# TensorE's instructions of five attention heads in a written order, with float32 values, an undivided attention map and transposed spreads

## The chip, the cores and the metric

One core of a Trainium2 chip runs the whole program as one launch. The metric is device time in microseconds (us), lower is better. Engines are named as the profile names them: PE is TensorE's matmul, PEld its weight load, DVE is VectorE, ACT is ScalarE, POOL is GpSimd, SPq is the queue of SyncE from which nearly all transfers are issued.

## The reference, cut to what matters

Two layers work on 512 tokens of width 1024. Layer 0 mixes with differential attention and a Fourier transform, layer 1 with a short convolution; after each comes a mixture of 16 experts that take 64 tokens each. What the change touches is the attention of layer 0 (6 heads, each with two maps of 64 channels, 768 keys of which 256 are context) and the vectors that modulate each layer (ada, 6 of 1024 per layer):

```python
s = jnp.einsum('bqhmd,bkhmd->bhmqk', q, k)
p = jax.nn.softmax(s, axis=-1)
a = p[:, :, 0] - lam * p[:, :, 1]
att = jnp.einsum('bhqk,bkhe->bqhe', a, v)
...
att = rmsnorm(att, subln) * (1.0 - lam_init)
o = jnp.concatenate([att, fourier_mix(f)], axis=-1)
return o @ w_out
...
sh_m, sc_m, g_m, sh_f, sc_f, g_f = split(silu(c) @ w_ada + b_ada)
```

## The kernel before, in words

The program runs in stages: the input and the first modulation (to about 94 us), heads 0 to 4 (about 94 to 344 us), head 5 with the output projection (to about 410 us), the choice of tokens for the experts (to about 449 us), experts of layer 0 (to 905 us), convolution and its choice of tokens (to 1145 us), experts of layer 1 (to 1608 us).

Matmuls of precision are written in two ways. A float32 matmul is one call of `mm` (L68) and stands in the trace as two PE instructions. `mm3` (L257) is three fp32r matmuls, each one instruction, on operands that `split` (L247 to L255) has cut into a high part (a cast on ACT, L250) and a low part (a difference on DVE, L251). A PE transpose is one instruction.

The head loop (`attention`, from L622) goes over `h` in 0 to 5 and over `i` in 0 to 3, the blocks of 128 queries; while head h is attended, head H = h+1 is projected. One round of `i` holds:
- `maxexp` (L461): for each of the two maps a DVE maximum over 768 keys (L466) and an ACT exponential (L467), which also gives the sums `su`.
- `proj(H, tt)`, two calls in each of the rounds 0 to 2: 24 fp32r matmuls of 384 columns (256 for the two context tiles), then `proj_fin` (L399): a square on ACT (L404), the split of v (L250, L251), the rotation on DVE (L409, L413, L424), the sum (L420), the root on POOL (L87, L88) and the product on POOL (L426).
- `scores(h, i+1)` (L450): 12 fp32r matmuls on half the rows of the array.
- `normalise` (L471): `lam / su1` on DVE, the second map scaled on ACT (L475), the first scaled and the second subtracted on DVE (L476).
- `proj_tr(H, i-1)` (L437): 4 transposes (2 for the context pair) of projected q and k, then splits.
- `att_tr` (L481): 6 transposes of the map, then `split` into `ah` and `al`.
- after odd rounds `values` (L494): 18 fp32r matmuls of 256 columns; in the next round `subnorm` (L506) sums the squares with matmuls against ones and takes the root on POOL, and `subscale` (L515) spreads the result over the partitions by a float32 matmul of a broadcast column with the identity.
- after round 3 the weights of head H+1 are loaded and split (`wsplit_head`); after heads 0 and 1 also `fourier` (L555): 8 float32 matmuls of 256 columns, a copy on ACT, 2 float32 matmuls of 512 columns.
- one step of `ada_steps` (L185): parts of a modulation vector (a load, ACT L170, DVE L174, POOL L176) and, after four parts, `ada_sum` (L178): 8 float32 matmuls of one column against ones.

No order is written: Tile's scheduler puts every engine's instructions in one fixed order at build time, by priority (the order of the program, shifted for ada parts by AP) and its own estimate of times. On the chip each engine works that order down, so an instruction that waits holds all behind it on its engine. Two banks of PSUM serve the tag `pj` (projections), two the tag `tr` (transposes, values, sums), four the scores. The tiles of a head's q, k and v come from the pool `qkv` with four slots, two for each head; head H takes the two that head h-1 had. The experts' weights are loaded from SPq into slots of several pools in a written cycle (`CYC`), among them the slots that attention gives back.

`gate_row` (L214) spreads a gate vector over the partitions with 8 float32 matmuls; it is called for both output projections and both choices of tokens.

Of the kernel before, what the change touches and what calls it, by code (L numbers as in the profile page):

```python
# [24 lines left out]
S = 512  # L25
# [17 lines left out]
def body(ctx: ExitStack, tc: tile.TileContext, t, out):  # L43
# [22 lines left out]

    def mm(o, l, r, start, stop):
        return T.matmul(o, l, r, start=start, stop=stop, skip_group_check=True)  # L68
# [47 lines left out]
    lam = cst.tile([128, 1], F32, name="lam")  # L116
# [14 lines left out]
    def small_params(raw, raw2):  # L131
# [13 lines left out]
        V.scalar_tensor_tensor(lam, le[:, 0:1], LAM0, le[:, 1:2], op0=ALU.add, op1=ALU.subtract)  # L145
# [32 lines left out]
    def ada_sum(l, w, acc):  # L178

        b = bank("tr", None)  # L180
        for k in range(KD):
            mm(b[:, k:k + 1], acc[:, k * 128:k * 128 + 128], one1, True, True)
        V.tensor_tensor(adaT[l, 0][:, w, :], b[:, :KD], biasT[:, l, w, :], op=ALU.add)

    def ada_steps(params, steps, new):  # L185

# [3 lines left out]
        for step in range(steps):  # L190
            while n < len(todo) and n * steps < (step + 1) * len(todo):
                l, w, j = todo[n]
                n += 1
                if j == 0:
                    if acc is not None:
                        ada_sum(*todo[n - 2][:2], acc)
                    acc = new()
# [4 lines left out]
        ada_sum(*todo[-1][:2], acc)  # L202
# [11 lines left out]
    def gate_row(l, which, pool_, after=None):  # L214

        dst = pool_.tile([128, D], F32, name=f"gate{l}{which}")
        for q in range(2):
            b = bank("tr", None)
            for k in range(4):
                m = mm(b[:, k * 128:k * 128 + 128],  # L220
                       adaT[l, 0][:, 2 + 3 * which, 4 * q + k:4 * q + k + 1].to_broadcast([128, 128]), ident,
                       True, True)
# [41 lines left out]
    def attention():  # L264
# [40 lines left out]
        sing = tabs.tile([128, NT, 2, 2, 64], F32, name="sing")  # L305
        gk1 = tabs.tile([128, 64], F32, name="gk1")
        gx_ = tabs.tile([128, 2, 64], F32, name="gx")

        def table_loads(st):
            gb = st.tile([128, 2, 64], F32, name="gb")  # L310
            SP.dma_start(out=cosg[:, :, 1, :], in_=t["cos"].rearrange("(a p) d -> p a d", p=128))
            SP.dma_start(out=sing[:, :, 1, 1, :], in_=t["sin"].rearrange("(a p) d -> p a d", p=128))
# [6 lines left out]
        def tables(gb):  # L319
            V.tensor_copy(gk1, gb[:, 1, :])  # L320
            V.tensor_scalar(gb[:, 0, :], gb[:, 0, :], 0.125, None, op0=ALU.mult)
            for b in range(4):
                V.tensor_copy(gx_[:, :, 16 * b:16 * b + 16], gb[:, :, 16 * (b ^ 1):16 * (b ^ 1) + 16])
            for j in range(2):
# [3 lines left out]
                for m in range(2):  # L328
                    V.tensor_tensor(sing[:, :, j, m, :], sing[:, :, 1, 1, :],
                                    gx_[:, j, None, :].to_broadcast([128, NT, 64]), op=ALU.mult)  # L330
# [56 lines left out]
        def new_head(h):  # L387
            a, b = [qkv.tile([128, 2048], F32R, tag="w", name=n) for n in ("qk", "qv")]
# [92 lines left out]
        def att_tr(h, i, p):  # L481
            if i % 2 == 0:
                AT[0] = [ap_.tile([128, 6, 256], F32R, tag=f"a{x}", name=f"a{x}") for x in "hl"]
# [869 lines left out]
```

## Time and profile before

| | |
|---|---|
| runs of the kernel before | 1604.41, 1606.08, 1611.53 us; median 1606.08 us |
| profiled execution | 1609.78 us; its span from first to last instruction 1608.0 us |
| busy share of the span | PE 94%, PEld 56%, DVE 42%, ACT 24%, POOL 14% |
| mean granted clock of TensorE | 0.979 |
| read from HBM | 491.41 MB |

The span is what the trace shows; the time of the execution has 1.8 us more around it. A busy PE is not a PE at its peak, since ends of matmuls are modelled and overlap; the distance from one start to the next tells what an instruction costs in a stream. The granted clock is 1.00 at 2.4 GHz and 0.50 at 1.2 GHz.

### The profile page before, as it was taken

The numbers are of one execution on the slowest core, as the hardware profiler recorded it, in microseconds if no ns is written. First come the engines' busy times: TensorE is split into PE (matmuls) and PEld (weight loads), VectorE is DVE, ScalarE is ACT, GpSimd is POOL, SyncE is SP. The second block draws the span as 40 slices with busy tenths as digits, with TensorE's granted clock in tenths as the row PEclk, the third lists the DMA queues.
The fourth block names the chain that finished last, engine by engine and source line by source line (L and its number), as shares of the span: only waits on it lengthen the run. The fifth ranks groups of instructions, "written<-read, shape, count | busy, mean of one in ns | idle before, by whom it ended". The sixth has DMA issues, their size and how long they took to land. (4 is left out here: it accounts for less than half of the span.)

```text
span 1608.0 us, 19864 instructions
## 1 busy us (share of the span) xinstructions
PE 1517.4 (94%) x7936; PEld 898.3 (56%) x7936; DVE 677.1 (42%) x1336; ACT 388.0 (24%) x753; POOL 225.3 (14%) x234
## 2 busy tenths in 40 slices
PE   4989999888999999999999899999899999999997
PEld 2978888777544444444443487887444444444443
DVE  3868788897612122112212567463312221221222
ACT  4535565553111001000100444232110010010000
POOL 0334355553000000000000024311000000000000
PEclk9889999999999999999999999999999999999999
DMA  9533444462799999999999766437999999999997
GB/s 346 168 103 106 156 136 155 158 236 104 302 364 360 410 409 409 409 409 409 409 409 404 265 209 209 157 131 271 348 399 399 409 409 409 410 408 409 409 409 278
DMA packets 162778, 494.79 MB, mean 308 GB/s; under 512 B 11750, under 2 KB 42879, under 8 KB 161663
## 3 DMA queue, kind: packets, MB, share of 16 engines
q1 hardware_dynamic: 161600, 491.23, 79.9%
q10 hardware_dynamic: 1086, 2.31, 0.4%
q8 instruction: 62, 1.02, 0.3%
q14 instruction: 30, 0.24, 0.0%
HBM read 491.41 MB, written 2.10 MB: 307 GB/s over the span
## 5 line engine op out<-in xcount | busy, mean ns | idle before, releaser
L1005 PE MATMUL s<-we,xs 128*64 128x512 f32 x1024 | 230.3, 597 | 0.0
L1005 PE MATMUL pj<-we,xs 128*64 128x512 f32 x1024 | 225.0, 593 | 4.5 <-DMA we<-in_moe_w_up_dram 4.5
L1005 PE MATMUL s<-we,aT 128*64 128x512 f32 x896 | 206.3, 603 | 0.0
L1005 PEld LDWEIGHTS pj<-we,xs 128*64 128x64 f32 x1024 | 75.6, 137 | 151.2 <-issue 140.8
L68 PEld LDWEIGHTS tr<-oh,x 128*128 128x128 f32 x1024 | 119.3, 191 | 50.2 <-issue 48.7
L1005 PEld LDWEIGHTS s<-we,xs 128*64 128x64 f32 x1024 | 69.3, 137 | 131.4 <-issue 125.8
L68 PE MATMUL tr<-oh,x 128*128 128x128 f32 x1024 | 131.2, 282 | 1.3 <-DVE oh L961 1.3
L1081 DVE TENSOR_TENSOR act<-act,pj 128x512 f32<-128x512 f32 x32 | 21.9, 688 | 261.3 <-PE pj L1005 240.3
L980 DVE TENSOR_SCALAR xs<-tr,am,ada 128x128 f32<-128x128 f32 x64 | 26.2, 409 | 230.4 <-PE tr L68 230.4
L1005 PEld LDWEIGHTS s<-we,aT 128*64 128x64 f32 x896 | 59.7, 137 | 103.2 <-issue 97.2
L1030 DVE TENSOR_TENSOR x<-x,tr 128x512 f32<-128x512 f32 x64 | 43.7, 685 | 139.8 <-PE tr L68 139.8
L176 POOL TENSOR_TENSOR ada<-ada,adaw 128x512 f32<-128x512 f32 x60 | 87.5, 1471 | 92.5 <-DVE adaw L174 45.4
L978 ACT ACTIVATE xs<-tr,ada,am 128x128 f32<-128x128 f32 x64 | 29.3, 458 | 273.2 <-DVE xs L980 273.2
L68 PE MATMUL pj<-whi,hh 128*128 128x384 f32 (+1 forms) x256 | 85.6, 334 | 0.3 <-ACT whi L250 0.3
L68 PE MATMUL pj<-wlo,hh 128*128 128x384 f32 (+1 forms) x256 | 83.1, 325 | 0.0
L68 PE MATMUL pj<-whi,hl 128*128 128x384 f32 (+1 forms) x256 | 83.0, 324 | 0.0
L1189 POOL TENSOR_TENSOR crs<-xsq 128x4 f32<-128x4 f32 x1 | 0.2, 203 | 485.2 <-ACT xT L1156 485.2
L1075 ACT ACTIVATE act<-s 128x512 f32<-128x512 f32 x32 | 17.4, 594 | 201.9 <-PE s L1005 168.3
L68 PE MATMUL pj<-chh,chi 128*128 128x512 f32 x160 | 62.4, 390 | 0.0
L68 PE MATMUL pj<-chl,chi 128*128 128x512 f32 x160 | 62.1, 389 | 0.0
L68 PE MATMUL pj<-chh,clo 128*128 128x512 f32 x160 | 62.0, 389 | 0.0
L710 POOL TENSOR_TENSOR wol<-wg,woh 128x512 fp32r<-128x512 f32 x32 | 47.2, 1489 | 96.6 <-ACT woh L709 91.7
(325 smaller groups left out, 2417.3 us busy)
## 6 DMA issues: line engine op xcount, KB each, us to landing
we<-in_moe_w_gate_dram SPq DMA_DIRECT2D x128, 1024.0 KB, 18.1
we<-in_moe_w_up_dram SPq DMA_DIRECT2D x128, 1024.0 KB, 18.2
we<-in_moe_w_down_dram SPq DMA_DIRECT2D x124, 1024.0 KB, 17.2
adaw<-in_ada_w_dram SPq DMA_DIRECT2D x48, 1024.0 KB, 5.6
cw<-in_conv_w_in_dram SPq DMA_DIRECT2D x12, 1024.0 KB, 6.4
wqk<-in_attn_w_in_dram SPq DMA_DIRECT2D x10, 512.0 KB
wo<-in_attn_w_out_dram SPq DMA_DIRECT2D x4, 1024.0 KB
we<-in_moe_w_down_dram SPq DMA_DIRECT2D x8, 512.0 KB
```

Source lines behind the costliest of these rows:

```text
L68: return T.matmul(o, l, r, start=start, stop=stop, skip_group_check=True)
L176: G.tensor_tensor(acc[:, cs], acc[:, cs], o, op=ALU.add)
L710: G.tensor_tensor(lo, wg, hi.bitcast(F32), op=ALU.subtract)
L978: A.activation(o_, i_, AF.Identity, bias=sh[:, kk:kk + 1], scale=am[:, kk:kk + 1])
L980: V.tensor_scalar(o_, i_, am[:, kk:kk + 1], sh[:, kk:kk + 1], op0=ALU.mult, op1=ALU.add)
L1005: pe(T.matmul(acc[hf][64 * j:64 * j + 64, :], lhs[:, 2 * kk + k, 64 * j:64 * j + 64], ws[j][:, k, hf * 512:hf * 512 + 512], start=kk == 0 ...
L1030: V.tensor_tensor(x1[tt][:, cs], src[tt][:, cs], b, op=ALU.add)
L1075: A.activation(act[:, hf * 512:hf * 512 + 512], ga[hf], AF.Silu)
L1081: V.tensor_tensor(act[:, cs], act[:, cs], up[hf], op=ALU.mult)
L1189: G.tensor_tensor(rs, xsq[:, :, 0], xsq[:, :, 1], op=ALU.add)
```

## The change

- From head 0 to head 4 every `mm` and every transpose of the heads (`turn`) is chained to the one before, so PE's order is that of the program text. The text's order changes with it: the second projection of a round moves from behind `att_tr` to behind `normalise`; `values` runs one round later, between the first projection and the scores (that of a head's second half in the first round of the next head); the end of `fourier` (`rest`) runs in the next head's first round; `subscale` precedes `proj_tr`.
- `ada_sum` becomes four float32 matmuls of 256 columns in four strips of 32 columns of the array, an ACT copy and two transposes, and runs at the start of a step instead of before the next vector's first part.
- Spreads (`subscale`, `gate_row`, the row of the convolution) become one transpose of a broadcast column instead of a float32 matmul.
- `values` uses float32 operands: 6 float32 matmuls instead of 18 fp32r; v and the transposed map are copied by ACT and no longer split.
- `normalise` forms p0 - lam*(su0/su1)*p1 without dividing by su0 and without the ACT pass; the norm that follows takes `EPS * su0^2` in place of `EPS`.
- The table `sing` loses its copy for the second map, and the rotation's product with it becomes two DVE instructions of half the size.

Outside the five ordered heads the scheduler orders PE as before. The core of the diff (renamings, the load of constants and the same spread in the convolution are left out):

```diff
+    def spread(o, col):
+        return T.transpose(o, col.to_broadcast([128, 128]), ident)
+    def inorder(m):
+        if order["on"]:
+            if order["last"] is not None:
+                tc.add_manual_dep(m.ins, order["last"].ins.name, NOSYNC, reason="the order of the heads")
+            order["last"] = m
+        return m
     def mm(o, l, r, start, stop):
-        return T.matmul(o, l, r, start=start, stop=stop, skip_group_check=True)
+        return inorder(T.matmul(o, l, r, start=start, stop=stop, skip_group_check=True))
+    def turn(o, i):
+        return inorder(T.transpose(o, i, ident))
...
         b = bank("tr", None)
-        for k in range(KD):
-            mm(b[:, k:k + 1], acc[:, k * 128:k * 128 + 128], one1, True, True)
-        V.tensor_tensor(adaT[l, 0][:, w, :], b[:, :KD], biasT[:, l, w, :], op=ALU.add)
+        for q in range(4):
+            T.matmul(b[32 * q:32 * q + 32, 0:256], one1.to_broadcast([128, 32]), acc[:, 256 * q:256 * q + 256],
+                     start=True, stop=True, skip_group_check=True, tile_position=(0, 32 * q))
+        A.copy(acc[:, 0:256], b[:, 0:256])
+        for c in range(2):
+            T.transpose(b[:, 256 + c * 128:384 + c * 128], acc[:, c * 128:c * 128 + 128], ident)
+        V.tensor_tensor(adaT[l, 0][:, w, :].rearrange("p (q c) -> p c q", c=2),
...
-            a, b = [qkv.tile([128, 2048], F32R, tag="w", name=n) for n in ("qk", "qv")]
+            a = qkv.tile([128, 2048], F32R, tag="w", name="qk")
+            b = slot("qv", qkv)
+            ql = ap_.tile([128, S], F32R, tag="ql", name="ql", bufs=2)
...
-            split(v[0][:, tt, :], v[1][:, tt, :], p[:, 256:384])
+            A.copy(v[:, tt, :], p[:, 256:384])
...
-        def normalise(p, su):
+        def normalise(i, p, su):
+            if i % 2 == 0:
+                AT["e"] = sm.tile([128, 2], F32, tag="e2", name="e2")
+            A.activation(AT["e"][:, i % 2:i % 2 + 1], su[:, 0:1], AF.Square, scale=EPS ** 0.5)
             rc = sm.tile([128, 2], F32, tag="rc", name="rc")
-            V.reciprocal(rc, su)
-            V.tensor_tensor(rc[:, 1:2], rc[:, 1:2], lam, op=ALU.mult)
-            A.activation(p[:, 1, :], p[:, 1, :], AF.Copy, scale=rc[:, 1:2])
-            V.scalar_tensor_tensor(p[:, 0, :], p[:, 0, :], rc[:, 0:1], p[:, 1, :], op0=ALU.mult,
-                                   op1=ALU.subtract)
+            V.reciprocal(rc[:, 0:1], su[:, 1:2])
+            V.scalar_tensor_tensor(rc[:, 1:2], su[:, 0:1], rc[:, 0:1], nlam, op0=ALU.mult, op1=ALU.mult)
+            V.scalar_tensor_tensor(p[:, 0, :], p[:, 1, :], rc[:, 1:2], p[:, 0, :], op0=ALU.mult, op1=ALU.add)
...
-                split(ah[:, i0:i0 + 3, qs], al[:, i0:i0 + 3, qs],
-                      b[:, :384].rearrange("p (i q) -> p i q", i=3))
+                A.copy(AT[0][:, i0:i0 + 3, qs], b[:, :384].rearrange("p (i q) -> p i q", i=3))
...
             for i in range(6):
-                mm3(o[:, :256], (v[0][:, i, :], v[1][:, i, :]), (ah[:, i, :], al[:, i, :]), i == 0, i == 5)
+                mm(o[:, :256], v[:, i, :], a[:, i, :], i == 0, i == 5)
...
-                mm(b[:, i * 128:i * 128 + 128], r[:, i:i + 1].to_broadcast([128, 128]), ident, True, True)
+                inorder(spread(b[:, i * 128:i * 128 + 128], r[:, i:i + 1]))
...
             H = h + 1 if h + 1 < NH else None
+            order["on"] = H is not None
             if H:
                 new_head(H)
             for i in range(4):
                 p, su = maxexp(s)
+                if H and i < 3:
+                    proj(H, 2 * i)
+                if due:
+                    pend = values(*due)
+                    due = None
+                if i < 3:
+                    s = scores(h, i + 1)
+                normalise(i, p, su)
                 if pend:
                     pend = subnorm(*pend)
                 if H and i < 3:
-                    proj(H, 2 * i)
-                if i < 3:
-                    s = scores(h, i + 1)
-                normalise(p, su)
-                if H and 0 < i:
-                    proj_tr(H, i - 1)
+                    proj(H, 2 * i + 1)
+                if rest:
+                    rest = rest()
                 if pend:
                     subscale(*pend)
                     pend = None
+                if H and 0 < i:
+                    proj_tr(H, i - 1)
                 att_tr(h, i, p)
+                if i % 2:
+                    due = h, i // 2, AT[0], AT["e"]
                 if H and i == 3:
                     s = scores(H, 0)
-                if H and i < 3:
-                    proj(H, 2 * i + 1)
-                if i % 2:
-                    pend = values(h, i // 2)
                 if not H:
+                    if due:
+                        pend = values(*due)
+                        due = None
                     wo.fill(i, fold_router)
                 if i == 3 and H and H + 1 < NH:
                     WH[H + 1] = wsplit_head(H + 1, wload_head(H + 1))
                 if i == 3 and h < 2:
-                    fourier(h)
+                    rest = fourier(h)
```

## Rows read from the trace of the kernel before

**Rows 1.** The page: its first line.
```profile
span 1608.0 us, 19864 instructions
```

**Rows 2.** Busy time by stage: heads 0-4, head 5, experts 0, convolution with routing.
```profile
core 0: us, PE busy (x) PEld busy (x) DVE busy (x) ACT busy (x) POOL busy (x), PEclk, DMA share, GB/s
94.00:344.00 250.00, 230.20 (x1529) 202.57 (x1529) 206.67 (x419) 142.60 (x303) 120.99 (x137) 0.97 0.44 147
...
344.00:410.00 66.00, 59.21 (x327) 48.48 (x326) 48.85 (x73) 24.92 (x49) 25.29 (x18) 0.97 0.40 147
...
449.00:905.00 456.00, 447.15 (x2239) 196.20 (x2239) 95.95 (x178) 45.59 (x85) 0.00 (x0) 1.00 1.01 399
905.00:1145.00 240.00, 229.08 (x1044) 180.81 (x1040) 144.58 (x265) 81.42 (x137) 54.01 (x41) 0.96 0.59 209
```

**Rows 3.** Waits of SPq's transfers, 300 to 530 us: total, times, longest.
```profile
SPq L154 <- PE s L1005: 67.8, 11, 17.0
```

**Rows 4.** Waits of PE, 94 to 344 us; the last line 344 to 410 us.
```profile
PE tr L489 <- DVE p L476: 5.3, 5, 1.6
PE tr L443 <- POOL qk L426: 4.2, 5, 1.2
PE tr L489 <- DVE qk L251: 3.4, 4, 2.3
...
PE tr L68 <- DVE al L251: 4.0, 2, 3.3
```

**Rows 5.** PE's instructions in order of time: start, us, line, what, count.
```profile
188.89 0.39 PE L68 MATMUL tr<-ah,qv 128*128 128x256 f32 x2
189.13 0.28 PE L68 MATMUL tr<-al,qv 128*128 128x256 f32 x1
...
189.36 1.02 PE L68 MATMUL pj<-dft,oT 128*128 128x256 f32 x4
190.22 1.02 PE L68 MATMUL pj<-four,bd_c 128*128 128x512 f32 x2
...
206.12 0.33 PE L68 MATMUL pj<-whi,hh 128*128 128x384 f32 x1
206.29 0.33 PE L68 MATMUL pj<-wlo,hh 128*128 128x384 f32 x1
...
257.33 0.97 PE L68 MATMUL s<-qk 64*128 64x512 f32 x8
...
258.59 0.66 PE L443 MATMUL tr<-ident,qk 128*128 128x128 f32 x4
...
264.70 0.85 PE L489 MATMUL tr<-ident,p 128*128 128x128 f32 x6 [1.25 <-DVE p L476]
265.31 0.36 PE L68 MATMUL pj<-whi,hh 128*128 128x256 f32 x1
...
328.19 1.95 PE L68 MATMUL tr<-ones,ada 128*128 128x1 f32 x16 [0.89 <-DVE al L251]
330.00 2.96 PE L68 MATMUL tr<-ident,ada 128*128 128x128 f32 x16
```

**Rows 6.** Groups of DVE instructions, 94 to 344 us: busy, mean ns, idle before.
```profile
L466 DVE TENSOR_REDUCE nm<-s 128x1 f32<-128x768 f32 x41 | 37.9, 947 | 0.7 <-PE s L68 0.4
...
L251 DVE TENSOR_TENSOR al<-tr,ah 128x384 fp32r<-128x384 f32 x40 | 21.7, 551 | 2.2 <-ACT ah L250 2.0
L476 DVE SCALAR_TENSOR_TENSOR p<-p,rc 128x768 f32<-128x768 f32 x20 | 21.6, 1080 | 5.5 <-ACT p L475 5.5
...
L413 DVE TENSOR_TENSOR t<-pj,sing 128x256 f32<-128x256 f32 x20 | 8.3, 413 | 0.0
```

**Rows 7.** Groups of ACT instructions, 94 to 344 us.
```profile
L467 ACT ACTIVATE p<-s,nm 128x768 f32<-128x768 f32 x41 | 37.1, 906 | 20.7 <-DVE nm L466 20.4
...
L475 ACT ACTIVATE p<-p,rc 128x768 f32<-128x768 f32 x20 | 18.8, 941 | 11.3 <-DVE rc L474 11.3
```

**Rows 8.** The root on POOL, a group of 0 to 560 us.
```profile
L88 POOL TENSOR_TENSOR qrs<-qrs,nhalf 128x4 f32<-128x4 f32 (+1 forms) x36 | 37.3, 1035 | 2.9
```

**Rows 9.** Busy time of one short stretch, columns as in group 2.
```profile
330.90:334.30 3.40, 3.15 (x16) 2.58 (x14) 3.40 (x5) 1.89 (x5) 3.32 (x3) 0.50 0.99 374
```

More of the change, by code (lines that the diff above doesn't have):

```diff
@@ L115, in body @@
     subg = cst.tile([128, 1], F32, name="subg")
[L116 removed]
+    nlam = cst.tile([128, 1], F32, name="nlam")
     def small_loads(st):
@@ L144, in small_params @@
         A.activation(le, pl[:, 0:2], AF.Exp)
-        V.scalar_tensor_tensor(lam, le[:, 0:1], LAM0, le[:, 1:2], op0=ALU.add, op1=ALU.subtract)
+        V.scalar_tensor_tensor(nlam, le[:, 1:2], LAM0, le[:, 0:1], op0=ALU.subtract, op1=ALU.subtract)
     def slot(name, pl=None):
@@ L190, in ada_steps @@
         for step in range(steps):
-            while n < len(todo) and n * steps < (step + 1) * len(todo):
+            if acc is not None and n % 4 == 0:
+                ada_sum(*todo[n - 1][:2], acc)
+                acc = None
+            while n < len(todo) and n * steps < (step + 1) * len(todo) and (acc is None or n % 4):
                 l, w, j = todo[n]
@@ L201, in ada_steps @@
             yield
-        ada_sum(*todo[-1][:2], acc)
+        while n < len(todo) or acc is not None:
+            if acc is not None and n % 4 == 0:
+                ada_sum(*todo[n - 1][:2], acc)
+                acc = None
+                continue
+            l, w, j = todo[n]
+            n += 1
+            if j == 0:
+                acc = new()
+            ada_part((l, w, acc), j)
         yield
@@ L566, in fourier, with rest @@
                 A.copy(fs[i].rearrange("p (m r) -> p r m", r=2), p.rearrange("p (r m) -> p r m", r=2))
-            p = bank("pj", None)
-            for i in range(2):
-                mm(p, fh["bd"][i], fs[i], i == 0, i == 1)
-            V.tensor_copy(oT[:, 6 + g, :], p)
+            def rest():
+                p = bank("pj", None)
+                for i in range(2):
+                    mm(p, fh["bd"][i], fs[i], i == 0, i == 1)
+                V.tensor_copy(oT[:, 6 + g, :], p)
+            return rest
         fr = {}
@@ L895, in route @@
         bc = bank("tr", None)
-        n = spread(bc, isel, 0)[1]
+        n = tokens(bc, isel, 0)[1]
         gs = tmp.tile([NE, 2, CAP], F32, name="gs")
@@ L910, in route, with tokens @@
         return gf, bc
-    def spread(b, isel, e):
+    def tokens(b, isel, e):
         return [mm(b[:, j * CAP:j * CAP + CAP], ident[:NE, e + j:e + j + 1].to_broadcast([NE, 128]),
@@ L956, in onehot @@
                 b = bank("tr", None)
-                for m in spread(b, isel, e):
+                for m in tokens(b, isel, e):
                     pe(m)
```

61 lines of the change are left out of this document (28 added, 33 removed).

## The prediction

> **What bounds the kernel now.** I read the page first, for the span [rows 1], then a table of busy time by stage [rows 2]. The experts of layer 0 last 456 us with PE busy 447 and the DMA share at 1.01. There PE and the stream of weights are both full, and the change touches neither. The stages that it touches are heads 0 to 4 (250 us, PE busy 230.2, DVE 206.7), head 5 (66 us, PE busy 59.2) and the convolution (240 us, PE busy 229). So time can only be won in the attention, before the experts begin, and some in the convolution. Does it reach the end? The expert stream starts as slots come free, and in 300 to 530 us its longest waits in total are for PE's expert matmuls [rows 3]; the earlier ones are for attention's work. If attention ends X us earlier, slots and PE come X earlier together. I pass X on in full; the bound below is that the stream moves by only half of it.
>
> Then PE's waits [rows 4] and its order of time [rows 5]. The waits named in heads 0 to 4 end with the map's subtraction (DVE L476), the product on POOL (L426) and the split of k (DVE L251); in head 5 4.0 us end with the split `al`. To see what is work, the steps from start to start serve [rows 5]:
> - a projection matmul of 384 columns: 206.29 - 206.12 = 0.17 us. One of 256 fp32r columns: (189.13 - 188.89) / 2 = 0.12.
> - a float32 matmul of 256 columns: (190.22 - 189.36) / 4 = 0.215 for each of its two instructions. From the same stretch the 512-column one costs twice that, 0.43 an instruction.
> - 12 score matmuls: 258.59 - 257.33 = 1.26. A transpose: (265.31 - 264.70) / 6 = 0.10. A float32 instruction against ones: (330.00 - 328.19) / 16 = 0.113.
>
> Work of one head: projections 96 x 0.172 + 48 x 0.12 = 22.3; scores 4 x 1.26 = 5.0; 34 transposes 3.5; values 2 x 18 x 0.12 = 4.3; norm sums and spreads 16 instructions, 1.8; ada sums, 4/3 a head, 2.4. Together 39.3, five times 196.5. The Fourier part of heads 0 and 1 adds 2 x (16 x 0.215 + 4 x 0.43) = 10.3. So 207 of the 250 us are work at full pace and 43 are lost: 20 as plain idle time [rows 2], the rest as broken streams, and stretches at 0.50 of the clock, that is at 1.2 GHz [rows 9], where PE had just waited 0.89 us and then run 16 one-column instructions [rows 5].
>
> **The change part by part.**
>
> *PE's work.* Values: 12 float32 instructions instead of 18 fp32r, 12 x 0.215 = 2.58 against 2.16, so +0.4 for each of 12 calls: +5 us, four of it in heads 0 to 4. Ada sums: 16 x 0.113 = 1.8 becomes two instructions deep in four strips, 2 x 0.215, and two transposes, 0.65 in all: -1.15 for each of ten (six in heads 0 to 4, one in head 5, three in the convolution). No row shows four strips side by side with 256 columns; if they did not overlap at all it would be 1.72 + 0.2, a loss of 0.1 each. I take 0.65, since 0.215 is what 256 columns cost. Spreads: two instructions of 0.113 become one transpose of 0.10: -0.125 each, 20 in heads 0 to 4, 4 in head 5, 8 in each gate row and 4 in the convolution. The two gate rows during the choice of tokens cost nothing before and win nothing, since PE waits there for DVE's top-k. In heads 0 to 4 this makes 4 - 7 - 2.5 - 1 (the gate row of the first output projection) = -6.5.
>
> *DVE and ACT.* The split `al` goes: 551 ns x 40 = 21.7 us of DVE's 206.7 [rows 6]. The split of v goes too. The ACT pass on the second map goes, 941 ns x 20 [rows 7], and with it one hop in the chain from maximum to map. The rotation's second product becomes two of half the size: between 0 and another 413 ns x 20 = 8 us of DVE [rows 6], taken as 4. The small square on ACT and the shorter table are costed at nothing: ACT is busy 142.6 of 250 [rows 2]. If that cover were gone, they would add some 0.2 us a round, 4 us. DVE comes down to about 180 of 250, so it frees PE rather than holding it.
>
> *The order.* From the end of scores to a map that can be transposed the chain is now two maxima (2 x 0.95), the second exponential (0.91) and its sum, small DVE steps and the subtraction (1.08) [rows 6, 7], some 4.6 us with the hops. In rounds 0 to 2 the written order puts scores, one projection or two (4.1 us each) and often the values between: 9 us or more. So these waits, L476's among them, should go. What is late next is the change of heads, round 3, which has no projections. `proj_tr` of the context tiles follows the last projection with only the spreads and transposes of 1.2 us between. Its chain is a square, a sum, the root on POOL (1.04 [rows 8]) and the product: 3 us or more, so PE waits 2. Then k is split before the next scores, 0.7, and the next projection waits for its weights, eight casts and eight differences that DVE does between the maxima: some 3. That is 6 us for each of five changes, 30 in place of 43. The written waits are hard: what stands behind a late `proj_tr` on PE is `att_tr`, the next scores and thus the next head. In rounds 0 of heads 1 to 4 the copy of v into head h-1's slot must wait for the late values; behind it on ACT stand squares and copies of the same projection, and PE has the other `pj` bank, so I cost it at nothing. If an exponential were queued behind it, it would cost the 2.6 us of the values each time.
>
> Heads 0 to 4: 207 - 5.5 + 30 = 231.5 against 250, and 1 for the gate row, rounded to -20 us. The bounds: nothing but the work, -6.5; no loss left at all, -49.
>
> *Head 5* is not ordered. Its 6.8 us of idle time (66.0 - 59.2) hold the 4.0 for `al`, which falls away [rows 2, 4]; values add 1.2, the ada sum and spreads give 1.6 back. -4, between 0 and -8.
>
> *Convolution.* Three ada sums -3.5, the gate row and spreads -1.5; the two transposes wait for an ACT copy of about 0.5 each time, +1. -4, between 0 and -5.
>
> *The number.* -20 - 4 - 4 = -28 on the profiled execution's 1609.8: 1582. That execution stands 3.7 above the median of 1606.1; the forecast is thus 24 under the median.
>
> A rule that speaks against the change stands in the Trainium skill, FP8 and Floating Point Precision, TensorE Precision Notes: true float32 takes four passes through the array. In our rows a float32 matmul of 256 columns costs 0.43 against 0.12 for an fp32r one, 3.6 times, so row and rule nearly agree. By four full passes values would cost 2.88 a call, and the sum would come out 4 us higher.
>
> **The rivals.**
>
> *Only the work goes* (chance 0.17). The order of the scheduler may already hide what can be hidden, and the waits move to the changes of heads. For it: PE's plain idle time is only 20 of 250 us, and DVE at 83% is near PE. Against it: 21.7 us of DVE's work leave. Price: -6.5 - 1 - 3 = -10, 1600.
>
> *The order does all that it can* (0.13). Half of the remaining 30 us goes too, since DVE's lower load lets the weights' splits run earlier: -45, 1565.
>
> *A slower kernel: changes of heads in a row* (0.10). PE stands still from the last projection until product, transposes, k's split, scores, maxima and weights' splits have run one behind the other: 3 + 0.7 + 1.3 + 2 + 5 = 12 us with 1.2 covered, and at 15 with DVE's queue in between, five changes lose 75 instead of 43. Place: round 3 of each head. For it: a fixed order cannot put ready work there, which the scheduler could. Against it: the fourier part fills it in two heads, and the next projection needs only the first of four parts of its weights. The price is +32 - 14 = +18, 1627. It decides from 71 us, 14 a change: then it outweighs the 28 won.
>
> *The clock* (0.07). In heads 0 to 4 the mean granted clock is 0.97 [rows 2]; in one stretch of 3.4 us it was 0.50, after a wait and 16 short instructions [rows 5, 9]. If the spreads as transposes and the stops at changes of heads made one more such stretch for each head and each choice of tokens, seven stretches would lose 1.7 each, 12 us: 1594. The Trainium skill, TensorE: Matmul & The Clock Gate, Part 4, says that a transpose does not count as busy in the way a matmul does; no row here separates the two.
>
> *The change doesn't do what it says* is in the first rival: as PE worked a fixed order before too, another fixed order can be worth nothing.
>
> **How the numbers follow.** The forecast case, 1582 with about 8 either way, has 0.53. The range for 8 in 10 goes from the good rival, 1563, through the case where the stream follows by half (1594), to just over the rival where only the work goes, 1604; left out are the slower one and parts of the two ends. A measurement of this kernel can tell about 0.5%, 8 us: under 1598 counts as faster. Faster: 0.53 + 0.13 + 0.07 and a quarter of the first rival = 0.77. Same: the rest of that rival, 0.13. Slower: 0.10.
>
> **What would show it.** Right: heads 0 to 4 take 225 to 237 us instead of 250, no wait for `al`, none or few for the map in rounds 0 to 2, and the longest PE waits lie in round 3, on the product of POOL L426 and on the weights; the experts of layer 0 keep their 456 us [rows 2] within 2. A values call takes 2.6 us, an ada sum 0.65 of PE. Wrong: PE waits in rounds 0 to 2 for the values' copies or the norm; heads 0 to 4 over 245 us; or a shorter attention with a longer experts stage, which would mean that the stream did not move with it.

## The result, and the profile after

The changed kernel takes 1615.25 us, the median of 20 runs, against 1605.13 us for 20 runs of the kernel before on the same chip. The ratio is 1.0058, with a 95% interval of 1.0046 to 1.0069: 9 us slower by the ratio, where 24 faster had been forecast. The profiled execution of after took 1618.38 us, its mean granted clock was 0.972 (0.979 before).

From the page of after, the span, to be set beside [rows 1], and the busy shares, beside the table of before:

```profile
span 1616.6 us, 19413 instructions
...
PE 1509.7 (93%) x7744; PEld 879.8 (54%) x7744; DVE 655.9 (41%) x1276; ACT 373.4 (23%) x763; POOL 214.0 (13%) x234
```

Every engine has less to do, and the span is 8.6 us longer. The busy time by stage, in the columns of [rows 2]: heads 0 to 4, head 5, experts of layer 0, convolution with routing. Stages begin elsewhere than before, so only the first is set against [rows 2] line by line (columns: us, then busy us and instructions of PE, PEld, DVE, ACT and POOL, granted clock, DMA share, GB/s).

```profile
91.40:347.70 256.30, 227.74 (x1407) 194.37 (x1406) 183.47 (x368) 130.28 (x309) 111.35 (x136) 0.94 0.42 140
347.70:416.00 68.30, 61.02 (x300) 47.93 (x301) 46.12 (x65) 22.49 (x50) 23.48 (x18) 0.93 0.41 145
466.00:915.00 449.00, 440.17 (x2199) 192.83 (x2196) 95.06 (x176) 44.64 (x83) 0.00 (x0) 1.00 1.02 402
915.00:1152.00 237.00, 220.12 (x985) 170.75 (x984) 148.63 (x265) 81.44 (x139) 53.52 (x41) 0.96 0.58 209
```

In heads 0 to 4 DVE fell from 206.7 us to 183.5 as worked out, and PE from 230.2 to 227.7. But the stage grew from 250 to 256.3: PE's plain idle time went from 19.8 us to 28.6, and its mean clock from 0.97 to 0.94. The stretches at half clock (0.50, 1.2 GHz) add up to 29.4 us there, 15.0 before, in one profiled execution of each.

Cut by the same events in every trace (the first exponential of heads 0 and 5, the first matmul that sums the routing's strips, `tr<-sel,oT`, the first gather matmul of each expert stage, the first convolution matmul), the stages last, in us:

| kernel | start | heads 0-4 | at half clock in them | rest of attention | routing | experts 0 | convolution, routing | experts 1 |
|---|---|---|---|---|---|---|---|---|
| before | 94.0 | 249.3 | 15.0 | 83.5 | 18.4 | 473.3 | 222.5 | 466.9 |
| after | 91.4 | 256.2 | 29.4 | 86.8 | 17.6 | 474.1 | 221.9 | 468.5 |

Heads 0 to 4 lose 6.9, the rest of the attention 3.3; the start, which no step of the forecast spoke of, wins 2.6, but it lies between 89.1 and 94.5 us in the profiles of this case, so little can be read into that. The experts' stages keep their length within 1.6, so what attention loses reaches the end.

PE's waits in heads 0 to 4 of after, longest sums first, to be set beside [rows 4] (line and engine waited for, us in all, times, longest):

```profile
PE tr L85 <- ACT at L525: 11.5, 16, 1.6
PE tr L85 <- DVE oT L550: 6.0, 6, 1.9
PE tr L85 <- DVE qk L283: 2.2, 4, 0.6
PE pj L82 <- ACT whi L282: 1.9, 1, 1.9
PE tr L82 <- ACT osq L534: 1.5, 1, 1.5
PE tr L69 <- POOL or L544: 1.0, 2, 0.8
```

The waits of [rows 4] on the map (5.3) and on POOL's product (4.2) are gone, and so is every wait on `al`. In their place stand 22 short ones, 17.5 us, on two readers of the `tr` banks: ACT's copy of the transposed map (L525) and DVE's scaled output (L550). This is how one of them arises, in PE's order of time, from the end of round 2 of head 2 through its round 3 (start, us, line, what, count, idle before):

```profile
230.74 0.43 PE L69 MATMUL tr<-ident,or 128*128 128x128 f32 x2 [0.20 <-POOL or L544]
231.01 0.60 PE L85 MATMUL tr<-ident,qk 128*128 128x128 f32 x4
231.74 0.55 PE L85 MATMUL tr<-ident,p 128*128 128x128 f32 x3
232.97 0.55 PE L85 MATMUL tr<-ident,p 128*128 128x128 f32 x3 [0.68 <-ACT at L525]
234.08 0.44 PE L85 MATMUL tr<-ident,qk 128*128 128x128 f32 x2 [0.57 <-ACT at L525]
234.36 0.49 PE L85 MATMUL tr<-ident,p 128*128 128x128 f32 x3
235.44 0.55 PE L85 MATMUL tr<-ident,p 128*128 128x128 f32 x3 [0.59 <-DVE qk L283]
235.92 0.50 PE L82 MATMUL s<-qk 64*128 64x512 f32 x2
```

Spreads, `proj_tr` and the two halves of `att_tr` all write to tag `tr`, which has two banks. Set back to back, nearly every group needs a bank that an earlier one of them has just filled, and PE waits until ACT or DVE has read it. These 20 transposes cost 2.0 us in a stream (0.10 each) and take 235.92 - 230.74 = 5.2 here. ACT's own order of time shows what a reader has ahead of it:

```profile
231.64 0.37 ACT L282 CAST qk<-tr 128x256 fp32r<-128x256 f32 x1
231.91 0.62 ACT L282 CAST whi<-wqk 128x512 fp32r<-128x512 f32 x1
232.43 0.48 ACT L525 COPY at<-tr 128x384 f32<-128x384 f32 x1
```

The copy takes 0.48 us, and ahead of it stand a cast of k and one of the next head's weights. The scheduler of the kernel before had set a projection, 4.1 us of PE, between such groups, as here behind the four transposes at 258.59 and ahead of the six at 264.70 [rows 5]:

```profile
259.00 0.42 PE L68 MATMUL pj<-whi,hh 128*128 128x384 f32 x1
```

The clock goes with it in part. Two pairs of neighbouring stretches of after, heads 0 and 4, columns as in [rows 2]:

```profile
124.20:127.60 3.40, 1.81 (x12) 1.15 (x11) 3.37 (x9) 3.33 (x11) 1.40 (x3) 1.00 0.00 0
127.60:134.40 6.80, 6.21 (x24) 4.55 (x23) 4.48 (x8) 2.22 (x6) 0.00 (x0) 0.50 0.46 152
329.00:332.40 3.40, 1.62 (x11) 0.91 (x9) 2.56 (x6) 2.04 (x6) 1.52 (x3) 1.00 0.86 255
332.40:342.60 10.20, 9.00 (x40) 5.95 (x41) 7.48 (x9) 6.12 (x13) 6.27 (x4) 0.50 0.75 254
```

After a stretch in which PE was busy for about half the time, at 2.4 GHz, it ran at 1.2 GHz for 6.8 and 10.2 us, although by then it had plenty of work (6.21 of 6.80 us and 9.00 of 10.20). That is not the only way into such a stretch: the one of before from 180.7 to 184.1 us follows 3.4 us in which PE was busy throughout.

### The profile page after: what moved, and what is told of

Read it like the earlier page. It is cut to its first block, busy times and chain, and to the rows that moved or that the text cites. A ratio compares the mean times of both kernels' runs of the same rounds, so it can differ in the third digit from the quotient of the medians.

```text
span 1616.6 us, 19413 instructions
## 1 busy us (share of the span) xinstructions
PE 1509.7 (93%) x7744; PEld 879.8 (54%) x7744; DVE 655.9 (41%) x1276; ACT 373.4 (23%) x763; POOL 214.0 (13%) x234
## 5 line engine op out<-in xcount | busy, mean ns | idle before, releaser
L191 DVE SCALAR_TENSOR_TENSOR adaw<-adaw,cin 128x512 f32<-128x512 f32 x60 | 53.1, 908 | 22.2 <-ACT adaw L187 21.9
## 6 DMA issues: line engine op xcount, KB each, us to landing
we<-in_moe_w_down_dram SPq DMA_DIRECT2D x124, 1024.0 KB, 17.5
```

Of the source, the lines that this page charges most:

```text
L191: V.scalar_tensor_tensor(o, s[:, 0, cs], cin[:, 0, j:j + 1], s[:, 1, cs], op0=ALU.mult, op1=ALU.add)
```

## The experiments

The theories. **A**: the written order puts users of the two `tr` banks in a row, and PE waits for their readers. **B**: transposes instead of matmuls (sums, spreads) lower the clock. **C**: the parts other than the order cost the time. Those that followed: **D**, PE work that is saved comes back as waits and as lower clock; **E**, the parts' costs add up; **F**, float32 values are dear; **G**, DVE is the bound; **H**, the chain from maximum to map is; **I**, the clock costs the time; **J**, the waits themselves do; **K**, with fp32r values the splits hold the banks; **L**, the parts help one another and the moved text is worth nothing to the scheduler; **M**, a part's price depends on the order it stands in. Ratios are to the kernel before on the same chip, with 95% intervals; the runs were spread over several chips, so two runs are compared by their ratios. Each has one profiled execution, and readings from it are of that execution.

**e1, the same text, but the scheduler orders PE.**

```diff
-            order["on"] = H is not None
+            order["on"] = False
```

> The changed kernel without the written order: the scheduler places PE's instructions again; text order, late values, float32 values, undivided map, new sums and spreads stay. Theory A (the written order puts users of the two tr banks back to back, so PE waits for each bank to be emptied, and the broken stream lowers the clock): waits of PE on the copy of the map and on the scaled output fall from 17.5 us in heads 0 to 4 to under 7, heads 0 to 4 take 240 to 250 us, ratio to the kernel before 0.992 to 1.001. Theory B (the clock falls because spreads and sums became transposes): the mean clock stays near 0.975 and the ratio at 1.003 or more. Theory C (the parts themselves cost more than reckoned, float32 values above all): ratio 1.004 to 1.008 as with the order.

Measured: 0.9982 [0.9968, 0.9996], median 1602.20 us of 12. So the written order itself costs 1.0058 / 0.9982 - 1 = 0.76%, 12 us. Heads 0 to 4 and PE's longest waits in them:

```profile
93.10:336.40 243.30, 226.90 (x1406) 192.44 (x1405) 177.62 (x367) 129.09 (x308) 113.82 (x136) 0.96 0.43 145
```

```profile
PE tr L85 <- DVE oT L550: 3.7, 2, 3.0
PE tr L85 <- ACT at L525: 3.3, 4, 1.2
PE tr L69 <- POOL or L544: 2.5, 2, 2.2
```

The waits on L525 and L550 fall from 17.5 us to 7.0, PE's idle time from 28.6 to 16.4, and its busy time hardly moves. A holds, at the edge of its "under 7"; B and C, which had 1.003 or more, fall.

**e2, written order, but spaced.** Each half of `att_tr` goes into the middle of a projection, so that in rounds 0 to 2 twelve projection matmuls stand on either side of it.

```diff
+                if k == 3 and mid:
+                    mid()
...
-                    proj(H, 2 * i + 1)
+                    proj(H, 2 * i + 1, lambda: att_tr(h, i, p, (0,)))
...
-                    proj(H, 2 * i)
+                    proj(H, 2 * i, half)
```

> The changed kernel, still in a written order, but the two halves of a map's transposes are set into the middle of two projections instead of back to back. Theory A: waits of PE on the copy of the map fall from 11.5 us to under 4, heads 0 to 4 from 256 to 232 to 246 us, mean clock up by 0.002 or more, ratio to the kernel before 0.985 to 0.999. Theory B: same number of transposes, so the clock stays near 0.975 and the ratio at 1.002 or more. Theory C: ratio 1.002 or more, since the parts are the same.

Measured: 0.9989 [0.9973, 1.0005], median 1603.20 of 12. Heads 0 to 4:

```profile
91.10:333.00 241.90, 222.55 (x1400) 192.60 (x1400) 183.13 (x368) 129.38 (x308) 114.44 (x136) 0.95 0.43 148
```

```profile
PE tr L85 <- ACT at L527: 3.3, 5, 1.0
PE tr L82 <- ACT osq L536: 3.2, 2, 2.9
PE tr L85 <- DVE qk L283: 2.7, 4, 0.8
```

The copy's wait (now L527) falls from 11.5 to 3.3 us, PE's idle time from 28.6 to 19.4 and the stage from 256.3 to 241.9, with the order still written by hand. That is theory A's test from its other side. One forecast of A missed: the mean clock was to rise by 0.002 and stayed at 0.9749 (0.9751 in the runs of after). So the 11 us between after and e2 went at an unchanged mean clock. A written order with the halves spaced is level with the scheduler's (their intervals overlap), not better.

**e3, spreads as matmuls again, in the changed kernel.**

```diff
-        return T.transpose(o, col.to_broadcast([128, 128]), ident)
+        return T.matmul(o, col.to_broadcast([128, 128]), ident, start=True, stop=True, skip_group_check=True)
```

> The changed kernel with the spreads as float32 matmuls again (two instructions of 0.113 us for one of 0.10), all else as changed. Theory A: nothing but the work comes back, 2.5 us in heads 0 to 4 and about 4 in all, ratio to the kernel before 1.005 to 1.010, clock unchanged within 0.001. Theory B: the mean clock rises by 0.003 or more and the ratio falls to 1.002 or less. Theory C: as theory A.

Measured: 1.0110 [1.0088, 1.0132], median 1623.31 of 5: 8 us slower than after, where A had 4. The mean clock was 0.9760 against 0.9751 in the runs of after. B falls for the spreads. The rule of the Trainium skill's page TensorE: Matmul & The Clock Gate, Part 4, that a transpose does not count as busy as a matmul does, shows no sign here: with matmuls in place of these 44 transposes the clock is 0.0009 higher, well inside the range of these five runs (0.974 to 0.979). The some 200 transposes of maps, q and k stayed, and no run here tests the rule on them.

**e4, the sums as eight one-column matmuls again, in the changed kernel.**

```diff
-        for q in range(4):
-            T.matmul(b[32 * q:32 * q + 32, 0:256], one1.to_broadcast([128, 32]), acc[:, 256 * q:256 * q + 256],
...
+        for k in range(KD):
+            T.matmul(b[:, k:k + 1], acc[:, k * 128:k * 128 + 128], one1, start=True, stop=True, skip_group_check=True)
```

> The changed kernel with a modulation vector's sum as eight float32 matmuls of one column again, at its new place. Theory A: up to 1.15 us for each of ten sums comes back, ratio to the kernel before 1.006 to 1.013. Theory B: two transposes fewer for each sum, clock up by 0.001 to 0.003, ratio 1.000 to 1.005. Theory C: if the strips and their wait for the copy on ACT cost more than the old form, the ratio is 1.004 or less.

Measured: 1.0126 [1.0103, 1.0149], median 1624.14 of 5, slower than after by 9 us (medians) or 11 (ratios), with a lower clock, 0.9718. B falls for the sums too. The forecast had priced all ten at 11.5.

**e5, the new sums and spreads alone, in the kernel before.** The edit is what the diff shown above has of `spread`, of `ada_sum` with its steps and of the three spreads (`subscale`, `gate_row`, the row of the convolution), and nothing else of it.

> The kernel before with two parts of the change alone: the sums in four strips and the spreads as transposes (11 us less work for PE). Theory D (in the heads PE's work is no longer what sets the time: the waits grow and the clock falls as PE gets idler, so work taken from PE is given back): ratio to the kernel before 0.996 to 1.002, mean clock 0.978 to 0.981 against 0.982. Theory E (parts add up: the two runs that put these parts back into the changed kernel cost 8 and 9 us): ratio 0.987 to 0.993.

Measured: 0.9970 [0.9954, 0.9986], median 1601.22 of 12. They win 5 us. By the prediction's prices their PE work is ten sums of 1.15 and 44 spreads of 0.125, 17 us. In the order of before two thirds of that saving does not arrive. D's forecast (0.996 to 1.002, clock 0.978 to 0.981) is met, with a clock of 0.9792; E's 0.987 to 0.993 is not.

**e6, float32 values alone, in the kernel before** (with the shorter table and the rotation in two halves, for without them the two float32 maps do not fit into the memory).

```diff
-                mm3(o[:, :256], (v[0][:, i, :], v[1][:, i, :]), (ah[:, i, :], al[:, i, :]), i == 0, i == 5)
+                mm(o[:, :256], v[:, i, :], a[:, i, :], i == 0, i == 5)
```

> The kernel before with the float32 values alone (v and map copied, not split; to make room the smaller table and the rotation's product in two halves come with them). Theory F (float32 values are the dear part: 5 us more of PE's work, and lower activity that lowers the clock): ratio to the kernel before 1.003 to 1.010, mean clock 0.975 to 0.979. Theory G (DVE is nearly the bound of the heads, and it loses 30 us of work): ratio 0.988 to 0.996. Theory D: 0.997 to 1.003.

Measured: 1.0035 [1.0019, 1.0050], median 1611.07 of 12: +5.6 us. The added PE work, priced at 5 in the forecast, would account for it alone. But the mean clock fell too, from 0.9813 to 0.9773, as F also had it, and the run does not separate the two. The 21.7 us of DVE that leave bring no gain that shows in the time (PE's idle time in heads 0 to 4 goes from 19.8 to 17.0 us). G falls, F holds.

**e7, the undivided map alone, in the kernel before.**

```diff
-            A.activation(p[:, 1, :], p[:, 1, :], AF.Copy, scale=rc[:, 1:2])
-            V.scalar_tensor_tensor(p[:, 0, :], p[:, 0, :], rc[:, 0:1], p[:, 1, :], op0=ALU.mult,
-                                   op1=ALU.subtract)
...
+            V.scalar_tensor_tensor(p[:, 0, :], p[:, 1, :], rc[:, 1:2], p[:, 0, :], op0=ALU.mult, op1=ALU.add)
```

> The kernel before with the undivided map alone (no ACT pass of 0.94 us between the exponential and the subtraction, one hop less). Theory H (the chain from the maximum to the map sets the rounds): up to 24 x 0.9 us goes, ratio to the kernel before 0.987 to 0.995. Theory D: 0.997 to 1.002, clock unchanged within 0.001.

Measured: 1.0028 [1.0008, 1.0048], median 1609.57 of 12. It takes 19 us of ACT's work and a hop out of the chain and is slower; neither D nor H had that. Heads 0 to 4, then PE's waits:

```profile
93.20:348.50 255.30, 235.28 (x1526) 207.26 (x1526) 207.95 (x419) 126.97 (x303) 119.14 (x137) 0.94 0.42 143
```

```profile
PE tr L443 <- POOL qk L426: 6.6, 5, 2.7
PE tr L491 <- DVE oT L520: 3.6, 3, 1.4
...
PE tr L491 <- DVE p L481: 0.3, 1, 0.3
```

The wait on the map went from 5.3 us to 0.3, as meant. PE's idle time is the same 20.0 us as before (19.8), since other waits have grown, the one on POOL's product from 4.2 to 6.6. What grew is PE's busy time on the same instructions, 230.2 to 235.3, as the stage's time at half clock went from 15.0 us to 30.8; the mean clock of the runs was 0.9761.

**e8, sums, spreads and undivided map in the kernel before** (the edits of e5 and e7).

> The kernel before with sums, spreads and the undivided map, without float32 values and without the written order. Theory E: the parts add up, ratio to the kernel before 0.980 to 0.990. Theory D: 0.994 to 1.001. Theory F: below the run with the order taken off (0.998) by 0.003 or more, since only the float32 values are missing.

Measured: 0.9974 [0.9958, 0.9990], median 1601.58 of 10. The undivided map on top of e5 costs 0.04%, against 0.28% alone; three intervals go into that difference, and they cover it. D's forecast is met; those of E (0.980 to 0.990) and F (0.003 or more below e1) are missed.

**e13, all four parts in the kernel before's own text and order** (the edits of e5, e6 and e7).

> All parts of the change (sums, spreads, undivided map, float32 values with the smaller table) on the kernel before, in its own text order and without a written order; against the run with the order taken off (0.998) only the late values, the late Fourier ends and the place of the second projection are missing. Theory E (parts add up from the single runs, 0.997 x 1.0035 x 1.003): ratio to the kernel before 1.001 to 1.006. Theory L (the parts help one another, and the moved text is worth nothing to the scheduler): 0.996 to 1.000; head 5 then takes 79 to 83 us, against 85 to 87 with the late values, since the last values of head 4 do not fall into it.

Measured: 1.0032 [1.0015, 1.0049], median 1611.13 of 12. The product of e5, e6 and e7 is 0.9970 x 1.0035 x 1.0028 = 1.0033: E holds in this order of the text within the noise, some 0.3% for such a product, and L falls. From here to e1 only the text moves (later values, later Fourier end, projections ahead), under the scheduler: 0.9982 / 1.0032 = 0.9950.

**e9, e2 with idle matmuls.** Three fp32r matmuls of 512 columns, whose result nobody reads, at two places in round 3 of heads 0 to 3, to keep the clock up.

```diff
+        def fill(p, n):
+            for _ in range(n):
+                mm(p, hh[:, 0, 0:128], hh[:, 0, 0:512], True, True)
```

> The spaced order with three idle fp32r matmuls of 512 columns (0.22 us each, their result is overwritten) set at two places of round 3 of heads 0 to 3, where PE waited for the projected q and k. Theory I (the waits at the change of heads lower the clock, and the clock takes back what the order wins): time at half clock in heads 0 to 4 falls from 26 us to under 16, mean clock from 0.975 to 0.978 or more, ratio to the kernel before 0.990 to 0.997 in place of 0.999. Theory J (the clock only follows the waits and costs little): 24 x 0.22 = 5 us of matmuls partly hidden in waits, ratio 0.998 to 1.003.

Measured: 0.9997 [0.9981, 1.0013], median 1604.23 of 12. The mean clock rose from 0.9749 to 0.9772, the time did not fall. J's forecast is met and all of I's are missed, but the test did not come about as planned: heads 0 to 4 were at half clock for 25.8 us in the profile, 26.4 in e2's. It does not tell I from J, also because the 24 added matmuls cost time of their own wherever no wait covered them.

**e11 and e12, e2 with fp32r values (split v and map, the long table), and the same with e9's idle matmuls.**

```diff
-                A.copy(AT[0][:, i0:i0 + 3, qs], b[:, :384].rearrange("p (i q) -> p i q", i=3))
+                split(ah[:, i0:i0 + 3, qs], al[:, i0:i0 + 3, qs],
+                      b[:, :384].rearrange("p (i q) -> p i q", i=3))
```

> The spaced order with values in three fp32r matmuls on split operands again (and the larger table and the undivided rotation of before); new sums, spreads, undivided map and late values stay. Theory F (float32 values cost, as alone: 1.0035): ratio to the kernel before 0.992 to 0.997 in place of 0.999, mean clock up by 0.002. Theory K (with the order spaced, DVE's splits hold the tr banks and the maxima longer, and PE waits): ratio 0.999 to 1.006.

> The spaced order with fp32r values and the idle matmuls of round 3 together. Theories F and I together: ratio to the kernel before 0.985 to 0.994, mean clock 0.979 or more. If only one of the two holds: 0.993 to 0.998. Theories J and K: 0.999 or more.

Measured: e11 1.0020 [1.0000, 1.0040], median 1606.22; e12 0.9999 [0.9984, 1.0014], median 1603.72, 12 runs each. In the spaced order fp32r values are not the cheaper ones. PE's waits in heads 0 to 4 of e11:

```profile
PE tr L85 <- DVE al L283: 9.1, 5, 3.3
PE tr L85 <- DVE p L514: 4.2, 3, 1.6
```

A bank is now held until a cast and a difference have read it, one behind the other on two engines, and PE waits 9.1 us for that: K. Idle matmuls took the clock from 0.9721 to 0.9772 and the time at half clock in heads 0 to 4 from 31.7 us to 17.6, and the median fell by 2.5 us; the two intervals overlap.

**e14, e1 with fp32r values (split v and map, the long table); e15, e14 with the divided map of before.**

```diff
 e14, against e1:
-                mm(o[:, :256], v[:, i, :], a[:, i, :], i == 0, i == 5)
+                mm3(o[:, :256], (v[0][:, i, :], v[1][:, i, :]), (a[0][:, i, :], a[1][:, i, :]), i == 0, i == 5)
 e15, besides:
+            A.activation(p[:, 1, :], p[:, 1, :], AF.Copy, scale=rc[:, 1:2])
```

> The changed kernel with the order taken off and the values in fp32r on split operands (with the larger table and the whole rotation of before); late values, new sums, spreads and undivided map stay. Theory E (parts add up, float32 values cost 0.0035 here too): ratio to the kernel before 0.993 to 0.996 in place of 0.998. Theory M (the late values go only with float32 operands, because the splits delay them or hold the banks): 0.998 to 1.004.

> As the run before, and the map divided again as in the kernel before; what stays of the change is the moved text, the new sums and the spreads. Theory E (the undivided map costs 0.003 here too): ratio to the kernel before 0.989 to 0.994. Theory M: the undivided map's saved pass is worth something once the order of the text has moved, ratio 0.998 to 1.005.

Measured: e14 0.9930 [0.9904, 0.9956], median 1593.35 of 7 runs (1589.38 to 1597.38): faster than both kernels, 11 us less than before by the ratio. e15 1.0005 [0.9988, 1.0021], median 1604.70 of 12. Heads 0 to 4 of e14:

```profile
94.00:335.00 241.00, 222.91 (x1470) 192.15 (x1467) 201.76 (x420) 130.89 (x309) 120.90 (x137) 0.96 0.45 150
```

Float32 values cost 0.9982 / 0.9930 - 1 = 0.52% here, 0.35% in e6, the same within the noise: E for that part. DVE is back at 201.8 us and the stage is no longer than e1's. The undivided map, a loss of 0.28% in e7, is worth 1.0005 / 0.9930 - 1 = 0.75% once the text is moved: M. How it does that is only half seen. Of the 12.3 us between the two profiled spans 4.3 lie in heads 0 to 4 and 2.3 in the rest of the attention, but 5.4 in the start, ahead of the first map (94.5 against 89.1), where e15's trace has 17.1 us at half clock and e14's 7.3.

## Why the prediction was wrong, step by step

**The bound.** Right: attention ends later by X and so does the kernel. Experts 0 last 474.1 us against 473.3. The eight loads that start the experts' gate weights, at 458.45 us before, come 8.1 later:

```profile
466.59 13.31 SPq L171 DMA_DIRECT2D we<-in_moe_w_gate_dram  x8
```

**PE's work.** Nearly right in size, instruction by instruction. A call of the values and an ada sum, in PE's order of time of after:

```profile
219.77 0.64 PE L199 MATMUL tr<-ada,ones 128*32 128x256 f32 x8
220.34 0.39 PE L82 MATMUL pj<-whi,hl 128*128 128x256 f32 x1
...
220.96 0.44 PE L203 MATMUL tr<-ident,ada 128*128 128x128 f32 x2
221.15 0.36 PE L82 MATMUL pj<-whi,hh 128*128 128x256 f32 x1
...
223.03 2.75 PE L82 MATMUL tr<-at,qv 128*128 128x256 f32 x12
225.71 0.50 PE L82 MATMUL s<-qk 64*128 64x512 f32 x2
```

The scores start at 225.71, so the values cost 225.71 - 223.03 = 2.68 us (2.58 forecast). The sum's strips take 220.34 - 219.77 = 0.57 (0.43), its transposes 0.19 (0.20). What such prices are worth in the kernel is another matter (e5). The price of four passes that the Trainium skill (FP8 and Floating Point Precision, TensorE Precision Notes) gives a float32 matmul would be 2.88 a call, an estimate; the measured 2.68 lies between it and the forecast.

**DVE and ACT.** The terms were right: `al` is gone, the map's subtraction costs about the same, the rotation a little more, as these groups of DVE in heads 0 to 4 of after show beside [rows 6].

```profile
L446 DVE TENSOR_TENSOR t<-pj,sing 128x128 f32<-128x128 f32 x40 | 9.5, 279 | 0.0
...
L515 DVE SCALAR_TENSOR_TENSOR p<-p,rc 128x768 f32<-128x768 f32 x20 | 22.6, 1129 | 0.5
```

What was read into them was wrong: "it frees PE rather than holding it". DVE at 83% had not held PE by its load: e6 takes the `al` work out and is slower by 5.6 us, and e14 puts it back and is the fastest of all. Where DVE does hold PE, as in e11, it is by a bank that it has not read yet.

**The order: the step that failed.** "So these waits, L476's among them, should go. What is late next is the change of heads, round 3, which has no projections." The first sentence came true for L476 and was read as if it held for all waits of rounds 0 to 2. The working followed the chains of operands (maximum to map, product to transposes) and asked of each whether a projection covers it. It asked this of no bank. `subscale`, `proj_tr` and the halves of `att_tr` stand together in the text, up to four groups in a round on two banks, and the prediction even put "only the spreads and transposes of 1.2 us" there as work that runs in a stream. The waits on L525 are 0.72 us each, those on L550 1.0; in PE's order of time 18 of the 22, 15.3 of the 17.5 us, lie at the `att_tr` of rounds 0 to 2. In place of "30 in place of 43" PE's plain idle time rose by 8.8 us. e1 and e2 take that away by two different means, and the stage falls to 243.3 and 241.9 us. The prediction had this as a sign of being wrong ("PE waits in rounds 0 to 2 for the values' copies or the norm; heads 0 to 4 over 245 us"), but for the operands of the values, not for the banks of the transposes.

This fault is 12 us, and forecast and measurement are 33 apart. The step's other half failed too: without the fault the stage is still 10 to 12 us above the forecast 231.5. Against the 201.5 us of work in the prediction's own sum (207 - 5.5) e1 and e2 still lose some 40 us, an estimate, where 30 were forecast and before lost 43. So the change, rid of the fault, takes away almost none of the loss that it was made for.

**The clock.** The rival was in the text with a chance of 0.07, and it priced seven more half-clock stretches at 12 us. Heads 0 to 4 have 14.4 us more at half clock, about 7 us if PE works through them, and 6.8 more after them (10.2 against 3.4 in the rest of the attention), 3 us. So the size was near. Of its two reasons e3 speaks against the spreads, and the change of heads is borne out: three of the five stretches that begin in heads 0 to 4 of after, 20.4 of 27.2 us, begin at 127.6, 284.6 and 332.4 us, in round 3 of heads 0, 3 and 4, behind the short waits there. The other two, 3.4 us each, begin at 253.9 and 305.1, right behind the two longest waits on L550 (1.7 and 1.9 us). Over the 20 runs of after, slower ones have the lower clock: about 0.9 us for each 0.001 (correlation -0.75; -0.87 over 33 runs of before). By that slope the difference of the mean clocks, 0.9813 (those 33 runs) against 0.9751, stands for 5.6 of the loss. That is a correlation; the idle matmuls, made to test it as a cause, settled nothing, and two results speak for a smaller share. e2 won the loss back at a mean clock of 0.9749. And heads 0 to 4 of e3, with 30.2 us of idle time, were at half clock for 19.9 us in place of 29.4 and took no less, 257.4 us, of which 2.5 are the spreads' added work by the prediction's price. Idle time and clock can't be priced as two separate items either: in the two pairs above the second follows on the first, though over the runs it need not (e7 has 20.0 us idle and 30.8 at half clock).

**Head 5.** -4 forecast, +3.3 measured for the rest of the attention. The wait for `al` is gone, but the map's copy has taken its place, and PE waits for the exponential and the norm besides. PE's waits in head 5 of after:

```profile
PE s L82 <- ACT p L501: 3.5, 1, 3.5
PE tr L82 <- ACT at L525: 2.8, 1, 2.8
PE tr L69 <- POOL or L544: 2.0, 2, 1.1
```

In all PE is idle there for 7.3 us, against 6.8 before, and the rest of the attention has 10.2 us at half clock, against 3.4. The late values of head 4, which now fall into head 5, are not what it takes: e13 and e6 have float32 values but no late ones, and the same stage took 85.7 and 85.8 us, with the same 2.8 us for the copy, where theory L in e13's expectation had 79 to 83 without them. In e8, with neither, it took 78.1. Over all profiles of this case it takes 84.7 to 89.1 us with float32 values and 78.1 to 84.6 with fp32r ones. So the loss goes with the float32 values.

**Convolution.** -4 forecast, -0.6 measured (222.5 to 221.9), though its PE work fell. The sums' saving did not come through there: e4, with the old sums, has 218.7, with 10.2 us of it at half clock, against 17.1 in after. Counted at full clock, an estimate, both come to some 213.5 us.

**The slower rival** had the right sign by another mechanism: at least 14 us lost at each of five changes of heads. No wait of PE in heads 0 to 4 is longer than 1.9 us, so it did not happen. With the fault out, e1 (0.9982) and e2 (0.9989) come nearest to the first rival, *Only the work goes*, and win less than its 10 us. One sum among the rivals is off: half of the 30 us on top of -28 is -43, 1567, not -45, 1565.

**As a sum.** The four parts in the old text cost 0.32% (e13), where the prediction had them as a gain: saved PE work came through by about a third, float32 values in full. The moved text under the scheduler wins 0.50%, and the written order loses 0.76%. Not settled: how much of the loss the clock causes; why the 40 us in heads 0 to 4 stay lost in e1 and e2; why the undivided map loses 0.28% in the text of before and is worth 0.75% in the moved one; and why the start, which this part hardly touches, is 5.4 us shorter in e14's profile than in e15's.

## What to carry to other kernels

Before writing an engine's order by hand, list for every short group its bank and that bank's reader, and keep as much other work between two uses of a bank as the reader takes: two banks and four groups in a row were a wait here, however early the operands were. An engine at 83% beside one at 92% is not the bound until a run that lightens it says so. Measure the parts alone and together and in each order: float32 values kept their price from one order to the other, the undivided map changed its sign.

## What was not expected of the hardware

- The clock fell after stretches in which PE was busy 1.6 to 1.8 of 3.4 us, with waits of only 0.27 to 0.75 us each, and stayed low for 6.8 and 10.2 us of nearly full work. In the kernel before it also fell once after 3.4 us of fully busy PE (from 180.7 us). Taking one wait out can lengthen the time at half clock: e7 went from 15.0 to 30.8 us with the same idle time.
- With idle matmuls the mean granted clock was higher by 0.0023 (e9, on another chip than e2) and 0.0051 (e12), but at most 2.5 us were won.
- A float32 matmul instruction of one column costs about as much as a transpose of 128: 0.113 us against 0.10 [rows 5]. In the changed kernel ten of the old sums cost 9 to 11 us more than four strips with two transposes (e4); part of that can be the lower clock.
